# Token-major residual and block-product gates in a two-layer hybrid encoder on one core

## The chip, the cores and the metric

The kernel runs on one core of a Trainium2 chip. The metric is device time in microseconds of one execution; lower is better. The core's engines work side by side, each through its own list of instructions in a fixed order: TensorE (PE; PEld is its weight load), VectorE (DVE), ScalarE (ACT), GpSimd (POOL) and SyncE (SP), which here only starts transfers between DRAM and the on-chip memory. TensorE writes into eight banks of accumulation memory (PSUM), each 128 x 512 f32; the other engines read them out.

## What is computed

512 tokens, model width 1024, two layers. `w_in` has 7424 columns: five groups of branch A, two of branch B, queries, keys and values of branch C, and 3 x 1024 gate columns.

```python
xn = rms_norm(x, ln1[l])
z = xn @ w_in[l]
a_q, a_i, a_ff, a_fb, a_g, b_u, b_v, c_q, c_k, c_v, gz = jnp.split(z, offsets, axis=-1)
o_a = hgrn2_bidirectional(a_q, a_i, a_ff, a_fb, lower[l])
y_a = rms_norm(o_a, a_norm[l]) * silu(a_g)
y_b = spatial_gating(gelu(b_u), gelu(b_v), w_s[l], b_s[l])
y_c = window_attention(qh, kh, vh, sink[l])
gates = sigmoid(gz.reshape(bsz, s_len, 3, D_MODEL))
merged = (gates[:, :, 0] * (y_a @ w_br[l, 0])
          + gates[:, :, 1] * (y_b @ w_br[l, 1])
          + gates[:, :, 2] * (y_c @ w_br[l, 2]))
x = x + merged @ w_out[l]
hn = rms_norm(x, ln2[l])
x = x + square(relu(hn @ w_up[l])) @ w_down[l]
```

After both layers comes `rms_norm(x, final_norm)`. Branch A is a gated linear recurrence, forward and backward, in four heads.

## The kernel before

Line numbers are those of the kernel before unless said otherwise. Activations lie feature-major: a tile holds 128 features by 512 tokens (`xT`, `xcur`, eight tiles for the width). Each f32 operand of a large product is split into a rounded part and a rest (`xh`, `xl`; `wh`, `wl`), and a product is three matmuls (`mm3`, L144): L145, L146, L147. Weights come in chunks of 128 x 1024 f32 (512 KB) through `wload` (L114): SP loads `wr`, ScalarE casts `wh` (L123), VectorE subtracts `wl` (L125). `wr`, `wh` and `wl` have two buffers each. `proj` (L149) makes one feature-major tile from one chunk, 24 matmuls. `proj_tok` (L158) makes four token-major tiles of 128 tokens by 512 features; a_i (`vt`) and b_v (`bv`) use it.

A layer goes: head 0 of branch A; branch B; head 1; branch C; heads 2 and 3; then `merge_pass` (L599) for each branch. `merge_pass` projects the gate columns (`gz`, L608), scales them with the row `rb` of norms (L611), takes a tanh (L612), projects the branch (`y`, L615) and multiplies (L619 to L622). Then follow the output projection `wo` (L794), the residual, the second norm, and the MLP in four parts `qd`: eight `up` projections, and a `down` (L289). `down` works by a scheme of seven block products in place of eight: sums of quarter blocks of the weights (L327, L340, L822, L825) and of the activations (`left_sums`, L251) go in, and `take` adds each product into `acc`. At the end of a layer `acc` is scaled, transposed (`dT`, L835) and added to `xcur`; the next norm's squares are summed over partitions by matmuls (`colsum`, `cs`, L188), the power is taken on POOL (L198), and `rb` is spread by matmuls (`bcast`, L205).

A head (`a_gates`, L384, and `a_head`, L415) is a chain. `a_gates` makes `ex` (one buffer) and `key`. Then seven levels: ScalarE takes two exponentials of `ex` (`qt` L437, `kt` L443), VectorE multiplies (L438, L445), TensorE makes `at` in a bank of the tag "a", of which there is one (L422), VectorE or ScalarE copies it under a mask (L427, L460), and VectorE updates `ex` four times (L464). After the levels come the states (`kd`, `kT`, `stp`, `st`), the output `av`, a norm, a transpose `oT` (L520) and the scaled copy (L522). Branch C goes through 16 pairs of a score step (`c_scores`, L704) and an output step (`c_out`, L734).

A scheduler fixes the order of each engine's list when the kernel is built: it takes the program, the dependencies and priorities (`tc.high_priority`), and mixes stages where buffers allow. So in the kernel before the matmuls of `gz` and `y` stand among those of heads 1 to 3 and branch C. Banks: 3 of tag "m", 1 "a", 2 "c", 2 "s".

Of the kernel before, what the change touches and what calls it, by code (L numbers as in the profile page):

```python
# [32 lines left out]
def trunk(tc, xT, ws, vec, bsb, snk, wst, rope, cmask, amask, ident, out):  # L33
# [17 lines left out]
    SLOTS = {"x": 16, "h": 22, "l": 12, "z": 4, "rb": 1, "q": 2, "a": 3, "oa": 4, "yc": 4, "g": 3}  # L51
    BRANCH = ("q", "a", "oa", "yc", "g")

    part = {}
    BANKS = {"m": 3, "a": 1, "c": 2, "s": 2}
    WR, WB, NZ, NCT, NSM, NQ = 2, 2, 3, 4, 4, 10
# [5 lines left out]
    def T(tag, name, dt=F32):  # L62
        where = part["br"] if tag in BRANCH else sb
        return where.tile([P, S], dt, tag=tag, bufs=SLOTS[tag], name=nm(name))

# [46 lines left out]
    ready = []  # L112

    def wload():  # L114
        if ready:
            return ready.pop(0)
        i = cnt[0]
        cnt[0] += 1
        with hp():
            raw = sb.tile([P, CW], F32, tag="wr", bufs=WR, name=nm("wr"))  # L120
            nc.sync.dma_start(raw, ws[i])
            hi = sb.tile([P, CW], F32R, tag="wh", bufs=WB, name=nm("wh"))
            nc.scalar.copy(hi, raw)  # L123
            lo = sb.tile([P, CW], F32R, tag="wl", bufs=WB, name=nm("wl"))
            nc.vector.tensor_tensor(lo, raw, hi.bitcast(F32), ALU.subtract)  # L125
        return hi, lo

    def qload():

        i = cnt[0]  # L130
        cnt[0] += 1
        t = part["mlp"].tile([P, CW], F32, tag="wq", bufs=NQ, name=nm("wq"))
        with hp():
            nc.sync.dma_start(t, ws[i])
        return t
# [13 lines left out]
    def proj(xs, name, w=None, koff=0, nk=KT):  # L149

        hi, lo = w if w is not None else wload()
        pt = PT("m", name)
        for k in range(nk):
            c = slice((koff + k) * P, (koff + k + 1) * P)
            mm3(pt, hi[:, c], lo[:, c], xs[k][0], xs[k][1], k == 0, k == nk - 1)
        return pt

    def proj_tok(xs):  # L158

        pts = [PT(tag, "pm") for tag in ("m", "m", "c", "c")]  # L160
        for i in range(4):
            hi, lo = wload()
            for k2 in range(2):
                k = 2 * i + k2
                c = slice(k2 * S, (k2 + 1) * S)
                for t in range(4):
                    tt = slice(t * P, (t + 1) * P)
                    xh, xl = xs[k][0][:, tt], xs[k][1][:, tt]
                    nc.tensor.matmul(pts[t], xh, hi[:, c], start=k == 0, stop=False)
                    nc.tensor.matmul(pts[t], xl, hi[:, c], start=False, stop=False)  # L170
                    nc.tensor.matmul(pts[t], xh, lo[:, c], start=False, stop=k == 7)
# [39 lines left out]
    def norm_begin(which, l):  # L211
        n = Norm()
        n.which, n.l, n.acc, n.last, n.xs, n.k = which, l, None, None, [], 0
        return n

    def norm_add(n, xt, do_split=True, sq_pool=False):
        k = n.k
        n.k += 1
        if do_split:
            hi, lo = T("x", "xh", F32R), T("x", "xl", F32R)  # L220
            split(xt, hi, lo, ln_ap(n.which, n.l, k))
            n.xs.append((hi, lo))
        sq = T("z", "sq")
        if sq_pool:
            nc.gpsimd.tensor_tensor(sq, xt, xt, ALU.mult)
        else:
            nc.scalar.activation(sq, xt, AF.Square)
        if n.acc is None:
            n.acc = sq
        elif not do_split and k == KT - 1:  # L230
            n.last = sq
        else:
            a = T("z", "sqa")
            nc.vector.tensor_tensor(a, n.acc, sq, ALU.add)
            n.acc = a

    def norm_end(n, square=False):
        rc = rstd_c(colsum(n.acc, n.last), D)
        n.rc = rc
        if square:  # L240
            n.src = SM("r2", 4)
            nc.vector.tensor_tensor(n.src, rc, rc, ALU.mult)
            return
        pt = bcast(rc)
# [3 lines left out]

    HT = 2 * P

    def left_sums(h, u, nh):  # L251

        V = nc.vector

        def hl(n):
            res = []
            for _ in range(n):
                if nh[0] < 22:
                    res.append(T("h", "sh", F32R))
                else:  # L260
                    res.append(part["mlp"].tile([P, S], F32R, tag="hx", bufs=6, name=nm("hx")))
                nh[0] += 1
            return res

        def two(pr, i):
            return tuple(x[:, i * HT:(i + 1) * HT] for x in pr)

        if h is None:
            p1 = hl(1)[0].rearrange("p (a b) -> p a b", a=2)
            split(u[:, 0:HT], p1[:, 0], p1[:, 1])  # L270
            sb_ = part["mlp"].tile([P, 2, HT], F32, tag="sf", bufs=2, name=nm("sf"))
            V.tensor_tensor(sb_[:, 0], u[:, 0:HT], u[:, HT:], ALU.subtract)
            return {1: (p1[:, 0], p1[:, 1]), "u": u, "s": sb_}
        v, u, sb_ = u, h.pop("u"), h.pop("s")
        v_ = hl(2)
        split(v, *v_)
        a11, a21, a12, a22 = u[:, 0:HT], u[:, HT:], v[:, 0:HT], v[:, HT:]
        sa = part["mlp"].tile([P, 2, HT], F32, tag="sf", bufs=2, name=nm("sf"))
        V.tensor_tensor(sa[:, 0], a22, a21, ALU.subtract)
        V.scalar_tensor_tensor(sa[:, 1], sa[:, 0], -1.0, a11, ALU.mult, ALU.subtract)  # L280
        a_ = hl(2)
        split(sa.rearrange("p a b -> p (a b)"), *a_)
        V.scalar_tensor_tensor(sb_[:, 1], a12, -1.0, sa[:, 1], ALU.mult, ALU.subtract)
        b_ = hl(2)
        split(sb_.rearrange("p a b -> p (a b)"), *b_)
        h.update({2: two(v_, 0), 4: two(v_, 1), 5: two(a_, 0), 6: two(a_, 1), 7: two(b_, 0), 3: two(b_, 1)})
        return h

    def down(qd, raw, hs, acc):  # L289
        b11, b12, b22, b21, t1 = raw[0:2], raw[2:4], raw[4:6], raw[6:8], raw[8:10]  # L290
        V = nc.vector
        first = qd == 0
# [15 lines left out]
        def take(t, fl, pt, sign, fresh=False):  # L308
            d = acc[t][fl]
            with hp():  # L310
                if fresh:
                    nc.scalar.activation(d, pt, AF.Copy, scale=float(sign))
                else:
                    V.tensor_tensor(d, d, pt, ALU.add if sign > 0 else ALU.subtract)

        pa = [PT("c", "dA") for _ in range(2)]
        product(1, b11, pa, True)
        for p in range(2):
            take(p, 0, pa[p], 1, first)
        pb = [PT("m", "dB") for _ in range(2)]  # L320
        product(2, b21, pb, True)
        for p in range(2):
            take(p, 0, pb[p], 1)
        t2 = b11
        with hp():
            for s_ in range(2):
                V.tensor_tensor(t2[s_], t1[s_], b22[s_], ALU.add)  # L327
        product(6, t2, pa, False)
        for p in range(2):
            take(2 + p, 0, pa[p], 1, first)  # L330
        pc = [PT("m", "dC") for _ in range(2)]
        product(7, b12, pc, True)
        for p in range(2):
            take(2 + p, 1, pc[p], -1, first)
        product(5, t1, pa, False)
        for p in range(2):
            take(2 + p, 1, pa[p], -1)
        with hp():
# [638 lines left out]
```

## Time and profile before

| | us |
|---|---|
| median of 3 runs | 1780.0 (1779.02 to 1781.77) |
| the profiled execution, its time | 1779.92 |
| the profiled execution, span from first to last instruction | 1778.1 |
| VectorE busy | 1251.2 |
| ScalarE busy | 947.4 |
| DMA traffic | 163.64 MB, mean 92 GB/s |

The page gives busy time as a share of the span, a strip of 40 slices in tenths, and groups of instructions by line: busy time, mean duration, and idle time ahead of them with what ended it. Matmuls are pipelined, so the durations of neighbours overlap.

### The profile page before, as it was taken

Reading aid. Unit: us, or ns where it says so; the run is one execution under the profiler, and the core shown is the slowest. Engines: PE = TensorE matmul, PEld = TensorE weight load, DVE = VectorE, ACT = ScalarE, POOL = GpSimd, SP = SyncE. Lnnn points to the kernel's source line nnn. Section 1 sums busy time; section 2 is a strip of 40 time slices with the busy share of each in tenths; the row PEclk is TensorE's granted clock in tenths of the full one; section 3 lists DMA queues with packets and bytes.
Section 4 is the critical chain, followed back from the end, with each engine's and each line's share of the span. In section 5 each row is a group of like instructions: output and inputs, shape, how many; then the busy total and the mean of one; then the engine's idle time right before and its main releaser. Section 6 shows DMA issues by size and latency. Waiting matters only on the chain.

```text
span 1778.1 us, 21652 instructions
## 1 busy us (share of the span) xinstructions
PE 1728.6 (97%) x8128; PEld 1426.8 (80%) x8128; DVE 1251.2 (70%) x2053; ACT 947.4 (53%) x1568; POOL 93.5 (5%) x105
## 2 busy tenths in 40 slices
PE   7999999999999999999999999999999999999995
PEld 5788888888778887878788877888878788888884
DVE  5678968675655758586867897777655556677675
ACT  3664876543335554546565669675323364645454
POOL 3012000000000000000110210000000000000000
PEclk9999999999999999999999999999999999999997
DMA  4222212222622232232132211122243223141401
GB/s 171 83 83 72 75 57 72 72 89 83 219 95 95 84 118 92 99 119 71 66 113 83 84 60 60 62 69 78 95 183 119 94 73 127 63 142 61 141 12 48
DMA packets 46728, 163.64 MB, mean 92 GB/s; under 512 B 5664, under 2 KB 6176, under 8 KB 46624
## 3 DMA queue, kind: packets, MB, share of 16 engines
q1 hardware_dynamic: 43488, 152.82, 25.4%
q0 software_dynamic: 2560, 8.39, 1.4%
q8 instruction: 64, 1.05, 0.2%
q10 hardware_dynamic: 576, 1.05, 0.2%
q14 instruction: 40, 0.33, 0.1%
HBM read 158.05 MB, written 4.19 MB: 91 GB/s over the span
## 4 chain that ended last, share of the span: by engine, by line
PE 85%; DVE 7%; ACT 5%; issue 1%; DMA 1%; SPq 0%; POOL 0%; DVEq 0%; ACTq 0%
PE up L145 7%; PE up L146 7%; PE up L147 7%; PE gz L145 5%; PE gz L147 5%; PE gz L146 5%; PE dA L304 3%; PE dA L306 3%; PE dA L305 3%; PE at L422 3%; PE y L145 2%; PE y L147 2%; PE y L146 2%; PE dC L304 2%; PE po L749 2%; PE wo L147 2%
## 5 line engine op out<-in xcount | busy, mean ns | idle before, releaser
L123 ACT CAST wh<-wr 128x1024 fp32r<-128x1024 f32 x220 | 229.7, 1049 | 362.4 <-PE up L146 104.9
L125 DVE TENSOR_TENSOR wl<-wr,wh 128x1024 fp32r<-128x1024 f32 x220 | 269.0, 1224 | 188.0 <-ACT wh L123 178.1
L145 PE MATMUL up<-xh,wh 128*128 128x512 f32 x512 | 199.7, 390 | 0.1
L147 PE MATMUL up<-xh,wl 128*128 128x512 f32 x512 | 199.4, 389 | 0.0
L146 PE MATMUL up<-xl,wh 128*128 128x512 f32 x512 | 199.3, 389 | 0.0
L139 ACT CAST wh<-wq 128x1024 fp32r<-128x1024 f32 x112 | 117.5, 1049 | 152.0 <-PE dA L305 44.1
L141 DVE TENSOR_TENSOR wl<-wq,wh 128x1024 fp32r<-128x1024 f32 x112 | 136.4, 1221 | 49.4 <-ACT wh L139 49.1
L145 PE MATMUL gz<-xh,wh 128*128 128x512 f32 x384 | 152.6, 397 | 2.7 <-ACT wh L123 2.2
L147 PE MATMUL gz<-xh,wl 128*128 128x512 f32 x384 | 151.5, 395 | 1.6 <-DVE wl L125 1.5
L146 PE MATMUL gz<-xl,wh 128*128 128x512 f32 x384 | 151.5, 395 | 0.0
L145 PEld LDWEIGHTS up<-xh,wh 128*128 128x128 f32 x512 | 96.1, 188 | 21.6 <-ACT wh L123 1.7
L147 PEld LDWEIGHTS up<-xh,wl 128*128 128x128 f32 x512 | 96.1, 188 | 19.9
L146 PEld LDWEIGHTS up<-xl,wh 128*128 128x128 f32 x512 | 96.1, 188 | 19.9
L145 PEld LDWEIGHTS gz<-xh,wh 128*128 128x128 f32 x384 | 72.5, 189 | 18.2 <-ACT wh L123 4.1
L147 PEld LDWEIGHTS gz<-xh,wl 128*128 128x128 f32 x384 | 72.5, 189 | 17.4 <-DVE wl L125 3.2
L464 DVE TENSOR_TENSOR ex<-ex 128x256 f32<-128x256 f32 x224 | 85.6, 422 | 0.2
L146 PEld LDWEIGHTS gz<-xl,wh 128*128 128x128 f32 x384 | 72.5, 189 | 13.6
L304 PE MATMUL dA<-wh,sh 128*128 128x512 f32 x208 | 81.9, 394 | 0.5
L305 PE MATMUL dA<-wh,sh 128*128 128x512 f32 x208 | 81.1, 390 | 0.0
L145 PE MATMUL y<-yh,wh 128*128 128x512 f32 x192 | 75.4, 395 | 3.4 <-DVE z L575 1.8
L147 PE MATMUL y<-yh,wl 128*128 128x512 f32 x192 | 75.9, 396 | 0.0
L146 PE MATMUL y<-yl,wh 128*128 128x512 f32 x192 | 75.4, 392 | 0.0
(312 smaller groups left out, 3987.2 us busy)
## 6 DMA issues: line engine op xcount, KB each, us to landing
wr<-in_ws_dram SPq DMA_DIRECT2D x220, 512.0 KB, 3.2
wq<-in_ws_dram SPq DMA_DIRECT2D x64, 512.0 KB, 3.3
x<-in_xT_dram SPq DMA_DIRECT2D x8, 256.0 KB, 9.1
xr<-in_xT_dram POOLq DMA_DIRECT2D x8, 256.0 KB, 4.0
xspill<-xr POOLq DMA_DIRECT2D x8, 256.0 KB, 2.8
xr<-xspill POOLq DMA_DIRECT2D x8, 256.0 KB, 3.0
out_dram<-xf SPq DMA_DIRECT2D x4, 256.0 KB, 2.4
out_dram<-xf ACTq DMA_DIRECT2D x4, 256.0 KB, 2.3
```

The lines of the kernel that those rows point to most:

```text
L123: nc.scalar.copy(hi, raw)
L125: nc.vector.tensor_tensor(lo, raw, hi.bitcast(F32), ALU.subtract)
L139: nc.scalar.copy(hi, raw)
L141: nc.vector.tensor_tensor(lo, raw, hi.bitcast(F32), ALU.subtract)
L145: nc.tensor.matmul(pt, whi, xhi, start=first, stop=False)
L146: nc.tensor.matmul(pt, whi, xlo, start=False, stop=False)
L147: nc.tensor.matmul(pt, wlo, xhi, start=False, stop=last)
L304: nc.tensor.matmul(pts[p], xh[:, t], hi[:, c], start=start and k == 0, stop=False, skip_group_check=True)
L305: nc.tensor.matmul(pts[p], xl[:, t], hi[:, c], start=False, stop=False, skip_group_check=True)
L306: nc.tensor.matmul(pts[p], xh[:, t], lo[:, c], start=False, stop=k == 3, skip_group_check=True)
L422: nc.tensor.matmul(pt[:, c], kk(st), qq[:, c], start=True, stop=True)
L464: nc.vector.tensor_tensor(ap_of(ex, o_, d), ap_of(ex, o_, d), ap_of(ex, i_, z), ALU.add)
```

## The change

- *Layout.* The residual, the branch outputs after projection, the sum over branches and the output projection become token-major: four tiles of 128 tokens by two halves of 512 features. Norm sums then lie along a row (`norm_tok`: ScalarE squares with a running sum); scaled transposes `xT` give the feature-major operands (`turn`). The sum over branches is transposed once (`mT`) ahead of `wo`. After the last layer the output is scaled and stored token-major.
- *Block products.* a_i beside b_v, and the three gates, are four units of 1024 x 1024. Each goes through `seven`, the scheme that `down` used, with sums of the normed input made by `left_x`. They stand ahead of the branches of their layer. A unit's weights come through `uload` into the ten `wq` buffers.
- *Gates in DRAM.* The tanh of each gate tile is stored to DRAM (`thd`) by a POOL-issued transfer and loaded again in `gated`, which takes the place of `merge_pass`.
- *Order.* b_u of layer 0 comes first. The projections `ag` and the splits of branch B come behind the heads in the program. In the MLP, `done` adds the residual and starts the next norm as the products of the last part come out.

```diff
+def _chunk_keys():
...
+        res += [(l, "bu", i) for i in range(4)]
+        res += [(l, "un", u, q, i) for u in range(4) for q in range(4) for i in range(2)]
...
+    GROUPS = (("m", "m", "c", "c"), ("m", "a", "s", "s"))
...
+    def uload(*key):
+        raw = []
+        for i in range(10):
+            t = part["wq"].tile([P, CW], F32, tag="wq", bufs=NQ, name=nm("wq"))
+            if i < 8:
+                with hp():
+                    nc.sync.dma_start(t, ws[CHUNK[key + (i // 2, i % 2)]])
+            raw.append(t)
+        return [raw[2 * q:2 * q + 2] for q in range(5)]
...
+    def norm_tok(which, l, xr, keep):
...
+        def add(t, fl):
+            j = T("jk", "jk")
+            nc.scalar.activation(j, xr[t][fl], AF.Square, accum_out=n.ss[:, t * 2 + fl:t * 2 + fl + 1])
...
+        def turn(fl, ts):
...
+                pt = PT("s", "xT")
+                for i, t in enumerate(ts):
+                    nc.tensor.transpose(pt[:, i * P:(i + 1) * P], xr[t][fl][:, (d % 4) * P:(d % 4 + 1) * P], id_t)
...
+    def left_x(n):
+        res = []
+        for k in range(4):
+            h = {1: two(n.xs[k], 0), 2: two(n.xs[k + 4], 0), 4: two(n.xs[k + 4], 1)}
+            left_sums(lambda: T("xs", "xs", F32R), h, n.xf[k], n.xf[k + 4])
+            res.append(h)
+        return res
+    def early_sums(raw):
+        b11, b12, b22, b21, t1 = raw
+        for i in range(2):
+            nc.vector.tensor_tensor(t1[i], b11[i], b12[i], ALU.add)
+        for i in range(2):
+            nc.vector.tensor_tensor(b12[i], b12[i], b22[i], ALU.add)
+    def seven(raw, hs, name, on):
...
+        pa = [PT("c", name + "A") for _ in range(2)]
+        product(1, b11, pa, True)
+        read("P1", pa)
+        pb = [PT("m", name + "B") for _ in range(2)]
+        product(2, b21, pb, True)
+        read("P2", pb)
...
+        product(6, b11, pa, False)
+        read("P16", pa)
+        pc = [PT("m", name + "C"), PT("a", name + "C")]
+        product(7, t3, pc, True)
+        read("P7", pc)
+        product(5, t1, pa, False)
+        read("P165", pa)
...
+        product(4, b21, pc, False)
+        read("P74", pc)
+        product(3, b22, pa, False)
+        read("P1653", pa)
...
+            def keep(z, t, fl):
+                nc.gpsimd.dma_start(thd[:, br * 4 + t, fl * S:(fl + 1) * S], z)
...
+                elif which == "P1653":
+                    z = T("zt", "zt")
+                    A.activation(z, pt, AF.Tanh, scale=sc[:, 4 + p:5 + p])
+                    keep(z, p, 1)
+                else:
+                    z = w.pop(({"P2": "P1", "P165": "P7", "P74": "P16"}[which], p))
+                    V.tensor_tensor(z, z, pt, ALU.add)
...
+                    A.activation(z, z, AF.Tanh, scale=sc[:, c:c + 1])
+                    keep(z, t, fl)
...
+        for u in range(4):
+            nxt = uload(l, "un", u + 1) if u < 3 else None
+            seven(raw, hx, "t" if u == 0 else "g", on_tok if u == 0 else on_gate(u - 1))
+            if nxt:
+                early_sums(nxt)
+            raw = nxt
...
-        merge_pass(0, yb)
...
+        def gated(bi, br, ys):
+            nonlocal grp
+            for fl in range(2):
+                th = []
+                for t in range(4):
+                    z = T("th", "th")
+                    nc.gpsimd.dma_start(z, thd[:, br * 4 + t, fl * S:(fl + 1) * S])
+                    th.append(z)
+                pts = proj_tok(ys, f"y{br}", (l, "y", br, fl), grp)
+                grp ^= 1
+                for t in range(4):
+                    with hp():
+                        if bi == 0:
+                            mg[t][fl] = T("mg", "mg")
+                            nc.vector.scalar_tensor_tensor(mg[t][fl], th[t], 1.0, pts[t], ALU.add, ALU.mult)
+                        else:
+                            nc.vector.scalar_tensor_tensor(th[t], th[t], 1.0, pts[t], ALU.add, ALU.mult)
+                            nc.vector.tensor_tensor(mg[t][fl], mg[t][fl], th[t], ALU.add)
+                if bi == 2:
+                    for d in range(4 * fl, 4 * fl + 4):
+                        pt = PT("s" if grp == 0 else "c", "mT")
+                        for t in range(4):
+                            nc.tensor.transpose(pt[:, t * P:(t + 1) * P], mg[t][fl][:, (d % 4) * P:(d % 4 + 1) * P], id_t)
...
+        def done(which):
+            def block(ts, fl):
+                for t in ts:
+                    nc.vector.scalar_tensor_tensor(xr[t][fl], acc[t][fl], r2[:, t:t + 1], xr[t][fl], ALU.mult, ALU.add)
+                    n1.add(t, fl)
+                    if not last:
+                        nc.gpsimd.dma_start(xspill[:, t, fl * S:(fl + 1) * S], xr[t][fl])
+                if not last:
+                    n1.turn(fl, ts)
...
+    for fl in (0, 1):
+        for t in (2, 3, 0, 1):
+            nc.vector.scalar_tensor_tensor(xr[t][fl], xr[t][fl], n1.rc[:, t:t + 1], fn_t[fl], ALU.mult, ALU.mult)
+            (nc.scalar if t % 2 else nc.sync).dma_start(out[:, t, fl * S:(fl + 1) * S], xr[t][fl])
```

In the changed kernel's order, as built, the four units of a layer stand first; then all `f`, `q`, `ck`, `cv` and `cq` projections ahead of the end of head 0; then, between the ends of heads 0 and 3, the `ag` projections, a part of the `y` products of branch B, and the small matmuls of heads and attention. Each SP list starts with the first weights and the `x` tiles; in the changed kernel the first eight `wq` loads stand among the `x` tiles.

664 lines of the change are left out of this document (349 added, 315 removed).

## The prediction

> **What bounds the kernel now.** I read the busy shares first, then the slices, then the windows between the ends of the recurrence heads, then the groups by line, and the order of instructions on each engine last.
>
> ```profile
> PE 1728.6 (97%) x8128; PEld 1426.8 (80%) x8128; DVE 1251.2 (70%) x2053; ACT 947.4 (53%) x1568; POOL 93.5 (5%) x105
> PE   7999999999999999999999999999999999999995
> DVE  5678968675655758586867897777655556677675
> ```
>
> TensorE is busy in every slice but the first and last, so fewer matmuls shorten the kernel as long as TensorE stays fed. The 70% of VectorE is a mean over unlike stages; the windows separate them (columns: length, busy time and count of PE, PEld, DVE, ACT, POOL, then granted clock, DMA share, GB/s). The inner borders at 157.7 to 448.3 and 1024.6 to 1306 are ends of heads (the scaled copy of `oT`, L522).
>
> ```profile
> 0.00:157.70 157.70, 142.94 (x672) 117.09 (x673) 111.66 (x192) 77.39 (x114) 26.77 (x29) 0.98 0.31 105
> 157.70:256.70 99.00, 97.36 (x509) 82.36 (x509) 82.55 (x189) 72.96 (x154) 10.49 (x11) 1.00 0.20 69
> 256.70:356.20 99.50, 99.50 (x528) 84.98 (x526) 74.34 (x170) 61.79 (x151) 4.36 (x6) 1.00 0.21 69
> 356.20:448.30 92.10, 91.96 (x455) 76.81 (x454) 59.68 (x98) 36.56 (x67) 2.87 (x3) 1.00 0.26 83
> 552.00:877.70 325.70, 325.33 (x1426) 264.92 (x1425) 226.34 (x293) 170.99 (x230) 1.15 (x1) 1.00 0.26 88
> 1024.60:1123.60 99.00, 93.39 (x488) 77.92 (x487) 83.70 (x196) 77.48 (x167) 8.05 (x7) 1.00 0.18 59
> 1751.00:1778.10 27.10, 9.06 (x49) 7.64 (x46) 14.17 (x21) 9.78 (x18) 4.44 (x3) 0.65 0.20 78
> ```
>
> Heads are VectorE's heaviest stage: 82.55 of 99.00 us (83%) and 83.70 of 99.00 (85%). TensorE is still full there, because the gate and branch projections (`gz`, `y`) lie between the heads' small matmuls. That cover is what the change takes away.
>
> **What a matmul costs.** Durations overlap, so I take distances between starts.
>
> ```profile
> 1180.29 0.39 PE L145 MATMUL gz<-xh,wh 128*128 128x512 f32 x1
> 1180.51 0.39 PE L146 MATMUL gz<-xl,wh 128*128 128x512 f32 x1
> ...
> 1183.38 1.02 PE L749 MATMUL po<-pT,cvt 128*128 128x256 f32 x4
> 1184.24 0.49 PE L744 MATMUL pT<-id_t,sc 128*128 128x128 f32 x3
> 1184.48 0.36 PE L715 MATMUL sc<-k,q 128*128 128x256 f32 x1
> 1184.68 0.28 PE L716 MATMUL sc<-kl,q 128*128 128x256 f32 x1
> 1184.80 0.39 PE L145 MATMUL gz<-xh,wh 128*128 128x512 f32 x1
> ...
> 1185.50 0.83 PE L485 MATMUL stp<-vt,kT 128*128 128x128 f32 x6
> 1186.09 0.47 PE L145 MATMUL gz<-xh,wh 128*128 128x512 f32 x1
> ```
>
> A 512-wide matmul takes 0.2275 us (0.22 and 0.23 alternate), a transpose 0.08, a plain f32 128-wide matmul 0.2 (it shows as two), one `po` 0.43, a score pair 0.32.
>
> **The change, part by part.** Fewer matmuls: the gates and a_i/b_v took 768 matmuls of 512 columns per layer. As seven block products per unit they take 4 x 7 x 24 = 672. Saved: 192 x 0.2275 = 43.7 us. Token-major residuals and gates need 160 transposes (96 `xT`, 64 `mT`) where 64 `dT` were: 96 x 0.1 = +9.6 at the rate of the tail. The column sums and one broadcast that go are worth about -5. Net on TensorE: -39.
>
> The tail:
>
> ```profile
> 1750.84 1.04 PE L835 MATMUL dT<-id_t,acc 128*128 128x128 f32 x8
> 1764.12 0.16 DVE L196 TENSOR_SCALAR ms<-cs 128x4 f32<-128x4 f32 x1 [3.73 <-PE cs L191]
> 1764.36 1.01 POOL L198 TENSOR_TENSOR rs<-ms,mhalf_t 128x4 f32<-128x4 f32 x1 [335.29 <-DVE ms L196]
> 1768.15 5.83 DVE L851 TENSOR_TENSOR xf<-xf,rb 128x512 f32<-128x512 f32 x6 [3.87 <-ACT rb L246]
> ```
>
> From the last product to the end are now 27.5 us. After the change the transposes, column sum and broadcast are gone: two accumulates and two residual adds (4 x 0.68), a square 0.7, sums 0.4, the power 1.0, eight multiplies 5.1, handoffs about 1, and the 4.1 us that now follow the last multiply (1773.98 to 1778.1): 15. Gain 12; between 8 and 15.
>
> The heads without cover are the step that decides. In the changed order, TensorE has `f`, `q`, `ck`, `cv` and `cq` of all heads ahead of the end of the first head, and between the ends of the first and the last head of layer 0 only 96 `ag` and 84 `y` matmuls of 512 columns, instead of the gates as well. Its work there: 180 x 0.2275 = 41, 144 f32 matmuls (at, av, stp) 29, 35 `po` 15, 100 transposes 8, 22 score pairs, half of them 384 wide, 9: 102 us. In layer 1, 106. VectorE's work between the same two markers (310 and 328 instructions) comes from these rows:
>
> ```profile
> L464 DVE TENSOR_TENSOR ex<-ex 128x256 f32<-128x256 f32 x224 | 85.6, 422 | 0.2
> L438 DVE TENSOR_TENSOR qt<-qt,q 128x512 f32<-128x512 f32 x56 | 39.5, 705 | 10.1 <-ACT qt L437 9.7
> L445 DVE TENSOR_TENSOR kt<-kt,key 128x512 f32<-128x512 f32 x48 | 32.9, 685 | 10.6 <-ACT kt L443 10.6
> L427 DVE COPY_PREDICATED at<-amask_t,at 128x512 f32<-128x512 uint8 x40 | 29.5, 738 | 12.3 <-PE at L422 12.3
> L718 DVE CUSTOM_DVE_ANT_0 sc<-sc,cmask_t,snk_t 128x256 f32<-128x256 f32 (+1 forms) x64 | 34.7, 544 | 16.3 <-PE pT L744 16.0
> L125 DVE TENSOR_TENSOR wl<-wr,wh 128x1024 fp32r<-128x1024 f32 x220 | 269.0, 1224 | 188.0 <-ACT wh L123 178.1
> ...
> 292.21 0.76 DVE L464 TENSOR_TENSOR ex<-ex 128x256 f32<-128x256 f32 x2
> ```
>
> Layer 0: 83 `ex` 35, 21 `qt` and 18 `kt` 27, 15 masked copies 11, 24 scores 13, 7 weight splits 9, some 140 others of their own forms 44: 139 us of durations. Two `ex` take 0.76 where 2 x 0.42 stand, so about 8% is overlap: 128 us. Layer 1: 135. So even a VectorE that never waits exceeds TensorE's 102 and 106 by 26 and 29, 55 us together: the lower bound. It will wait, though: `ex` has one buffer, and the `at` bank is one, so a head's seven levels and its tail run in series, each crossing ScalarE, VectorE and TensorE, and the next head queues behind. VectorE's share in these stages is 85% at best and 65% at worst (59.68 of 92.10). At 65% the excess is 95 + 102 = 197, the upper bound. I take 85%, nearest to the head that runs beside the attention: 128/0.85 - 102 = 49 and 135/0.85 - 106 = 53, together +101. The stretch up to the end of the first head stays under TensorE: layer 0 has 433 matmuls of 512 columns there, 98 us, and 21 us of small ones, against 93 us of VectorE's rows.
>
> Smaller terms, with the rows that price them:
>
> ```profile
> 5.88 1.22 DVE L125 TENSOR_TENSOR wl<-wr,wh 128x1024 fp32r<-128x1024 f32 x1 [4.94 <-ACT wh L123]
> 11.63 1.23 DVE L125 TENSOR_TENSOR wl<-wr,wh 128x1024 fp32r<-128x1024 f32 x1 [3.09 <-ACT wh L123]
> ...
> 10.00:15.00 5.00, 3.19 (x7) 1.91 (x8) 3.37 (x3) 4.26 (x7) 3.17 (x2) 1.00 1.06 407
> ...
> xr<-xspill POOLq DMA_DIRECT2D x8, 256.0 KB, 3.0
> ...
> L612 ACT ACTIVATE gz<-gz 128x512 f32<-128x512 f32 x48 | 30.2, 628 | 3.5 <-DVE gz L611 3.4
> ```
>
> Start: SP now issues eight 512 KB `wq` loads between the `x` loads, and VectorE has four wide sums (1.22 each), ten half-width differences and four splits ahead of the last `xl`, some 13 us more; the 3.09 us that it waits after its first weights and a little besides take 4 of it, so +9 (0 to 13). Layer boundary: the transposed splits, 16 differences and eight splits for the sums, about 23 us of VectorE, must precede the third product; two products cover 11, and today's loss there is 2: +10 (0 to 14). Branch to gated sums: gate tiles come back from DRAM into space the heads free, 3 us per load, and eight multiplies of 0.68 must release a bank group before the next projection: +4 a layer, +8 (0 to 20). Unit to unit: the last product's two banks wait for two tanh of 0.63: 1.2 x 6, +7 (0 to 15).
>
> Costed at nothing: within a unit, 14 splits and 8 sums x 1.22 plus 6 adds x 0.68 are 31 us on VectorE against 168 x 0.2275 = 38 on TensorE, as in the window 552 to 877.7, where the MLP products run at 226.34 of 325.70 with TensorE full. Without that cover each unit would cost what VectorE lacks. The gates' way through DRAM adds 24 writes and 24 reads of 256 KB per layer; a unit then moves 4.2 MB of weights and 2.1 MB of gates in 38 us, 165 GB/s, and 407 were reached at the start. POOL issues these transfers in order with its own work, and the powers queued behind them are waited for at stage ends only.
>
> Sum, against the profiled execution's span: 1778.1 - 39 - 12 + 101 + 9 + 10 + 8 + 7 = 1862, plus the 1.8 us by which its time (1779.92) exceeds its span: 1864. That execution lies at the median, 1780.0. I round to **1862**.
>
> **Rivals.** (1) *TensorE stays the bound.* The heads' idle time stays below the 51 us saved, because VectorE's rows there shrink once no gate work is mixed in and the heads overlap each other: 1779.9 - 51 = 1729 with no idle time, some 1740 with a little. For it: 97% busy now, and 51 us that are certain. Against: the 55 is a sum of rows. It decides from the point where TensorE's added idle time, both layers, is under 51 us. Chance 0.10.
>
> (2) *The clock falls.* After TensorE sat idle, the same rows get slower:
>
> ```profile
> 1760.54 1.84 PE L188 MATMUL cs<-ones_t,sqa 128*128 128x1 f32 x8 [3.99 <-DVE sqa L234]
> 552.57 0.95 PE L188 MATMUL cs<-ones_t,sqa 128*128 128x1 f32 x8
> ```
>
> 1.84 against 0.95 for the same eight, clock 0.65 in the last window. If the gaps in the heads do this throughout, the work of 102 and 106 doubles to 204 and 212, over VectorE's 151 and 159: +106, 1970; for half of the time about 1915. Against: the heads' small matmuls come every microsecond or two. Chance 0.15. The Trainium skill ("TensorE: Matmul & The Clock Gate", "Part 1: The HAM clock gate") says that TensorE is throttled to half clock by default and after an idle window of about 3.4 us; the 3.99 us gap agrees with it, and by that rule the gaps that I expect would leave the clock up.
>
> (3) *The gates' return is the wait.* POOL's queue lets the loads go late, and each of the six gated groups of a layer waits for a landing of 3 us plus its multiplies, 12 x 6 = 72 in place of my 8: 1926. Against: eight buffers, loads ahead of use. Chance 0.05.
>
> **How the numbers follow.** Forecast 0.70, rivals 0.10, 0.15, 0.05. The forecast's own range is 1815 to 1915: its idle term at 100% (1818) up to near 72%. The range for eight in ten takes the floor with the small terms at nothing (1784) and half of the clock case with a few terms high: 1784 to 1930. About 0.2% is what a measurement can tell from no change. Faster by that needs rival 1: 0.10; within it 0.03; slower 0.87.
>
> **What would show it.** Right: TensorE busy 20 to 40% less than the length of the stretch between the first and last head ends (about 150 us long against 290 now), VectorE near 85% there, `at` and `qt` rows waiting for each other, and no idle time in the block products beyond a microsecond a unit; a tail near 15 us. Wrong: TensorE above 90% busy there, VectorE's rows shorter than today's, or the idle time in the block products or at the gate loads instead. A clock well under 1 in these stretches speaks for rival 2, idle time of `mg` rows behind DMA for rival 3.

## The result and the profile after

The changed kernel takes 1921.28 us (median of 4 runs, 1918.14 to 1922.46) against 1779.85 us for the kernel before beside it: ratio 1.079, 95% interval 1.0772 to 1.0809, so slower. The prediction was 1862: right in sign, and 59 us too low. The measured time lies 6 us beyond the forecast's own range (1815 to 1915) and inside its range for eight in ten (1784 to 1930). All line numbers below are those of the kernel whose rows are shown.

The page of the changed kernel, its busy times and three of its strips of 40 slices:

```profile
PE 1773.7 (92%) x7984; PEld 1435.0 (75%) x7984; DVE 1386.0 (72%) x2206; ACT 1028.4 (54%) x1707; POOL 142.6 (7%) x199
...
PE   6999999688699999999989999987887999999997
...
DVE  8887688677574676676887758986865657576867
...
PEclk7999999699699999999989999997997999999999
```

TensorE has 144 instructions fewer than before (7984 against 8128) and is busy for longer (1773.7 against 1728.6 us). The strip shows where: two dips of the PE line, slices 8 to 11 and 27 to 31, with lower digits of the granted clock under them. The windows put borders to that. Their columns are those of the prediction's windows; 340.2, 404.8, 465.2, 520.6 and 1283.1, 1348.2, 1411.3, 1464.8 are ends of the four heads of each layer (scaled copy of `oT`, L598).

```profile
0.00:48.40 48.40, 30.31 (x88) 20.38 (x88) 39.65 (x71) 23.49 (x35) 14.67 (x17) 0.79 0.61 223
48.40:218.70 170.30, 166.78 (x713) 133.24 (x714) 132.41 (x145) 97.49 (x123) 15.17 (x26) 0.99 0.32 108
218.70:340.20 121.50, 119.96 (x599) 100.45 (x597) 98.15 (x183) 74.78 (x123) 16.91 (x16) 1.00 0.28 91
340.20:404.80 64.60, 48.68 (x216) 40.72 (x217) 42.75 (x81) 29.62 (x54) 3.19 (x4) 0.74 0.10 33
404.80:465.20 60.40, 48.65 (x278) 38.57 (x277) 49.09 (x165) 48.76 (x151) 4.79 (x5) 0.97 0.03 9
465.20:520.60 55.40, 39.75 (x191) 33.20 (x190) 28.94 (x64) 22.59 (x59) 1.02 (x1) 0.77 0.06 20
520.60:623.60 103.00, 100.17 (x445) 80.94 (x446) 63.05 (x85) 33.20 (x49) 17.50 (x32) 0.97 0.48 169
...
966.20:1138.30 172.10, 166.74 (x701) 131.09 (x700) 132.73 (x153) 99.79 (x142) 19.48 (x29) 0.97 0.35 117
...
1464.80:1567.70 102.90, 100.63 (x444) 81.42 (x445) 63.11 (x85) 33.18 (x49) 17.16 (x32) 0.97 0.48 169
...
1907.20:1920.70 13.50, 0.00 (x0) 0.00 (x0) 7.75 (x14) 1.39 (x4) 1.01 (x1) 0.67 0.40 156
```

The stages that the prediction kept full are full: the block products (166.78 of 170.30) and the stretch of the first head (119.96 of 121.50). From the first to the last head end of layer 0 it is otherwise, and there VectorE is not full either: 42.75 of 64.60, 49.09 of 60.40, 28.94 of 55.40. The same two markers for both layers in one row each:

```profile
340.20:520.60 180.40, 137.09 (x682) 112.48 (x682) 120.79 (x308) 100.98 (x263) 8.99 (x10) 0.83 0.07 21
1283.10:1464.80 181.70, 136.94 (x702) 112.95 (x700) 123.61 (x318) 114.36 (x282) 8.89 (x10) 0.85 0.06 21
```

They last 362.1 us together. VectorE's share is 67% and 68%, where 85% had been taken. TensorE's 137 us are longer than its 102 and 106 us of work, in part because its mean clock was at 0.83 and 0.85: divided by that, the work would be 123 and 125 us. What makes up the rest was not traced.

VectorE's rows themselves kept their size (`ex`, now L540: 87.4 us against 85.6), and `at` waits for `kt`, as had been named. Two groups by line:

```profile
L498 PE MATMUL at<-qt,kt 128*128 128x128 f32 x448 | 75.5, 321 | 42.5 <-DVE kt L521 37.8
...
L540 DVE TENSOR_TENSOR ex<-ex 128x256 f32<-128x256 f32 x224 | 87.4, 434 | 0.1
```

Inside head 1, VectorE's rows of a level and the first of the next:

```profile
351.58 0.69 DVE L514 TENSOR_TENSOR qt<-qt,q 128x512 f32<-128x512 f32 x1 [0.69 <-ACT qt L513]
352.19 0.72 DVE L503 COPY_PREDICATED at<-amask_t,at 128x512 f32<-128x512 uint8 x1
352.80 0.68 DVE L521 TENSOR_TENSOR kt<-kt,key 128x512 f32<-128x512 f32 x1
353.39 1.43 DVE L540 TENSOR_TENSOR ex<-ex 128x256 f32<-128x256 f32 x4
355.52 0.69 DVE L514 TENSOR_TENSOR qt<-qt,q 128x512 f32<-128x512 f32 x1 [0.69 <-ACT qt L513]
```

A level comes every 3.94 us (351.58 to 355.52). VectorE waits in it once, 0.69 us for ScalarE's exponential, so it is busy for 3.2 of 3.94, 82%: near the 85%. The tail of a head is another matter. Head 3 of layer 0, TensorE's and VectorE's rows behind the last level:

```profile
500.12 2.07 PE L498 MATMUL at<-qt,kt 128*128 128x128 f32 x8 [2.53 <-DVE kt L521]
...
504.49 1.65 PE L561 MATMUL stp<-vt,kT 128*128 128x128 f32 x6 [0.57 <-ACT kT L558]
507.29 0.90 PE L556 MATMUL kT<-id_t,kd 128*128 128x128 f32 x3 [1.15 <-DVE st L568]
...
510.45 0.29 DVE L564 COPY st<-stp 128x128 f32<-128x128 f32 x1 [3.21 <-PE stp L561]
...
517.30 0.17 DVE L222 TENSOR_SCALAR ms<-ss 128x4 f32<-128x4 f32 x1 [5.79 <-ACT asq L589]
518.60 0.69 DVE L592 TENSOR_TENSOR ao<-av,rs 128x512 f32<-128x512 f32 x1 [1.13 <-POOL rs L224]
...
519.43 1.09 PE L596 MATMUL oT<-id_t,ao 128*128 128x128 f32 x4 [3.35 <-DVE ao L592]
```

and the window over them:

```profile
498.20:520.60 22.40, 12.79 (x50) 10.55 (x50) 6.92 (x17) 6.26 (x22) 1.02 (x1) 0.58 0.00 0
```

Every row waits for another engine, and each engine waits in turn; VectorE is busy for 6.92 of the last 22.4 us (31%). So a head without cover is some seven levels at VectorE's pace, and then some 20 us in which no engine is the bound. Head 1's tail is not bare in this way: the 96 `ag` projections stand among its steps in TensorE's order, and its second `kT` starts 11.7 us after its first `stp` (370.45 to 382.14), where head 3 takes 2.8 (504.49 to 507.29).

### The profile page after: what moved, and what is told of

It reads as the page before. It is cut to its first block, busy times and chain, and to the rows that moved or that the text cites. A ratio compares the mean times of both kernels' runs of the same rounds, so it can differ in the third digit from the quotient of the medians.

```text
span 1920.7 us, 22066 instructions
## 1 busy us (share of the span) xinstructions
PE 1773.7 (92%) x7984; PEld 1435.0 (75%) x7984; DVE 1386.0 (72%) x2206; ACT 1028.4 (54%) x1707; POOL 142.6 (7%) x199
## 3 DMA queue, kind: packets, MB, share of 16 engines
q10 hardware_dynamic: 576, 1.05, 0.1%
## 4 chain that ended last, share of the span: by engine, by line
PE 58%; issue 20%; DVE 13%; ACT 6%; DMA 1%; SPq 0%; POOL 0%; POOLq 0%; DVEq 0%; ACTq 0%
PE up L172 3%; PE up L170 3%; PE up L171 3%; PE gA L377 2%; PE gA L375 2%; PE gA L376 2%; PE y L197 2%; PE y L195 2%; PE at L498 2%; PE y L196 2%; DVE wl L166 2%; DVE ex L540 2%; PE wo L195 2%; PE wo L197 2%; PE wo L196 2%
## 5 line engine op out<-in xcount | busy, mean ns | idle before, releaser
L166 DVE TENSOR_TENSOR wl<-wq,wh 128x1024 fp32r<-128x1024 f32 x224 | 273.8, 1224 | 141.3 <-ACT wh L164 134.5
L164 ACT CAST wh<-wq 128x1024 fp32r<-128x1024 f32 x224 | 234.9, 1049 | 255.2 <-PE dA L376 54.0
L166 DVE TENSOR_TENSOR wl<-wr,wh 128x1024 fp32r<-128x1024 f32 x156 | 193.4, 1239 | 173.5 <-ACT wh L164 169.8
L164 ACT CAST wh<-wr 128x1024 fp32r<-128x1024 f32 x156 | 163.5, 1049 | 267.0 <-PE up L171 107.9
L498 PE MATMUL at<-qt,kt 128*128 128x128 f32 x448 | 75.5, 321 | 42.5 <-DVE kt L521 37.8
L498 PEld LDWEIGHTS at<-qt,kt 128*128 128x128 f32 x448 | 68.4, 228 | 50.2 <-issue 31.7
L377 PE MATMUL dA<-wl,sh 128*128 128x512 f32 x256 | 90.6, 394 | 0.0
L540 DVE TENSOR_TENSOR ex<-ex 128x256 f32<-128x256 f32 x224 | 87.4, 434 | 0.1
L195 PE MATMUL y<-wh,yh 128*128 128x512 f32 x192 | 79.8, 415 | 2.4 <-ACT on L598 1.6
L196 PE MATMUL y<-wh,yl 128*128 128x512 f32 x192 | 78.3, 408 | 0.0
L197 PE MATMUL y<-wl,yh 128*128 128x512 f32 x192 | 72.7, 407 | 1.6 <-DVE wl L166 1.6
```

The costliest lines, as they stand in the source:

```text
L377: nc.tensor.matmul(pts[p], xh[:, t], lo[:, c], start=False, stop=k == 3, skip_group_check=True)
L498: nc.tensor.matmul(pt[:, c], kk(st), qq[:, c], start=True, stop=True)
```

## The experiments

Twelve kernels, each an edit of the changed one (1921) or of the one named. e1_cover, e7_nounit, e10_align and e12_al are medians of four runs; the other eight are single runs, and the four runs of the changed kernel itself lie 4.3 us apart, so that a difference of 3 or 4 us in a single run shows nothing by itself. Theories: A, the heads' series of steps lost its cover; B, VectorE's amount of work; C, the gates' way through DRAM; D, the lower clock; E, the token-major parts; F and G, the start address of tiles or not.

| run | edit | us |
|---|---|---|
| e1_cover | gates beside the branches again | 1858.3 (1.0446, 1.0428 to 1.0463 against before) |
| e7_nounit | no block products ahead of the branches | 1803.3 (1.0125, 1.0108 to 1.0142) |
| e3_two | doubled buffers in a head, splits of branch B later | 1885.1 |
| e2_fill, e6_fill2, e13_tailclk | unread matmuls that hold the clock | 2019.2, 1947.3, 1911.1 |
| e5_nodram | gate tiles not stored and loaded | 1924.9 |
| e4_start | first weights started by POOL | 1918.2 |
| e11_half, e12_al | tiles moved by 384 and 128 bytes | 1908.6, 1908.5 (1.0725, 1.0707 to 1.0744) |
| e10_align | e7_nounit, tiles moved by 384 bytes | 1793.1 (1.0079, 1.0064 to 1.0094) |
| e14_sum | e3_two, e12_al and e4_start together | 1866.0 |

### The cover: e1_cover and e7_nounit

```diff
-        res += [(l, "un", u, q, i) for u in range(4) for q in range(4) for i in range(2)]
+        res += [(l, "un", 0, q, i) for q in range(4) for i in range(2)]
...
-        gated(0, 1, ys)
+        merge_pass(0, 1, yb, None)
```

> The changed kernel with one part undone: only a_i and b_v go as block products; the gates are projected feature-major beside the branch projections again, as before, without the way through DRAM; the token-major output projection, residual, MLP end and tail stay. Theory A (the heads lost their cover: their chain runs in series through single buffers and leaves TensorE idle about 154 us over both layers): 1921 - 154 idle + 144 x 0.2275 = 33 of matmuls that come back - 6 for 64 transposes mT that go = about 1795, between 1775 and 1815, and TensorE above 95% busy between the head ends. Theory B (VectorE is the bound between the head ends by the mere amount of its work): the gate rows come back onto VectorE there (24 scalings and 24 sums of 0.68 a layer), so this stretch gets no shorter than the work it then holds, and the whole stays above 1850. Theory C (the gates' way through DRAM is the wait): also near 1795, but the gain would have to stand at the gated sums, not between the heads.

Measured: 1858.3, half of what theory A expected. Its windows between the head ends of layer 0:

```profile
223.90:289.00 65.10, 50.77 (x216) 42.48 (x217) 39.33 (x76) 28.85 (x52) 3.23 (x5) 0.70 0.08 25
289.00:399.50 110.50, 110.50 (x584) 94.39 (x584) 79.72 (x201) 71.73 (x181) 4.02 (x5) 1.00 0.20 67
399.50:477.60 78.10, 75.28 (x381) 61.65 (x379) 53.41 (x97) 37.31 (x76) 3.55 (x6) 1.00 0.20 66
```

The first gate matmul, and TensorE's row ahead of it:

```profile
254.38 1.65 PE L563 MATMUL stp<-vt,kT 128*128 128x128 f32 x6 [0.57 <-ACT kT L560]
257.20 0.79 PE L172 MATMUL gz<-xh,wh 128*128 128x512 f32 x1 [1.18 <-DVE q L627]
```

Heads 2 and 3 are full again. Head 1 is as bare as in the changed kernel (65.1 us, clock 0.70): the one unit of block products ahead of head 0 had taken 45 us (48.6 to 93.7) in which no head ran, the `f`, `q` and `cq` projections were used up under head 0 alone, and the gates began only at 257.2, behind head 1's levels in TensorE's order and after a last wait of 1.18 us for VectorE's scaling of a `q`. So cover counts only where it stands beside the chain. Theory B's number, above 1850, came true, but not by its way: VectorE was busy for 39.33 of the 65.10 us of head 1, and heads 2 and 3, with the gate rows back on VectorE, are TensorE's.

e7_nounit takes the last unit out too:

```diff
-        for u in range(1):
-            seven(raw, hx, "t" if u == 0 else "g", on_tok)
+        vt = tok_tiles("vt", "vt", 0)
...
+        bv = tok_tiles("bv", "bv", 0)
```

> The changed kernel without any block products ahead of the branches: a_i, b_v and the gates are projected where the kernel before has them, head 0 starts at once, its b_u projection stands behind it again; the token-major output projection, residual, MLP end and tail stay. Theory A (the projections are the cover of the heads' chain, and block products ahead of head 0 use them up): TensorE above 95% busy from head 0 to the last head, and against the kernel before only the tail (-14), column sums (-5) and 32 more transposes (+3), and what wo and the MLP took longer in e1_cover (+8 a layer, the transposes among it): 1765 to 1785. Theory E (the token-major parts themselves cost what e1_cover is slower than before): 1820 or more.

```profile
154.90:440.60 285.70, 276.96 (x1421) 232.54 (x1420) 209.44 (x445) 165.84 (x357) 18.52 (x19) 0.99 0.20 68
1048.00:1336.60 288.60, 273.59 (x1385) 229.06 (x1385) 209.41 (x448) 174.63 (x366) 16.03 (x17) 0.98 0.20 66
```

Measured: 1803.3, 118 us under the changed kernel although 192 matmuls come back, with TensorE at 97% and 95% between the head ends. (The edit also takes out the costs of the units at the start and at their edges, so the 118 us are not the cover's alone.) The tail, 13.2 us, is the changed kernel's. It stays 23 us above the kernel before and 18 above the expectation: of these e10_align (below) explains 10, and the rest was not traced. Theory E, 1820 or more, falls.

### Single buffers: e3_two

```diff
-    BANKS = {"m": 3, "a": 1, "c": 2, "s": 2}
+    BANKS = {"m": 2, "a": 2, "c": 2, "s": 2}
...
-        ex = part["br"].tile([P, 4, S], F32, tag="ex", bufs=1, name=nm("ex"))
+        ex = part["br"].tile([P, 4, S], F32, tag="ex", bufs=2, name=nm("ex"))
```

> The changed kernel with the single buffers of a head doubled: bank tag a from 1 to 2 (m from 3 to 2), ex and at from one buffer to two, z2 from 3 to 4, the tag of qt and kt from 3 to 5; for the room, the splits of branch B come behind the last head (some 3 us a layer). Theory A (single buffers put heads in series): two heads run side by side, the stretch between first and last head end falls from 180 towards VectorE's 128 and 135 us of work, the whole by 40 to 90 us, to 1830-1880. Theory B (VectorE's amount of work): within 10 us of 1921.

```profile
319.00:477.80 158.80, 129.87 (x712) 108.94 (x710) 122.40 (x329) 111.48 (x285) 6.74 (x8) 0.92 0.10 34
1236.10:1411.00 174.90, 138.78 (x742) 116.08 (x740) 137.50 (x364) 129.60 (x315) 6.67 (x8) 0.92 0.10 31
```

Measured: 1885.1, 36 us less, just outside the weak end of what theory A named. The two stretches fall from 180.4 and 181.7 to 158.8 and 174.9 us, and VectorE's share rises from 67% and 68% to 77% and 79%. But TensorE's order changed with the edit, and the 36 us can't be put down to the buffers alone. Ahead of the end of head 0 stand 341 and 422 of the layer's projections of 512 columns in place of 432 and 522, and the stretches up to there, from the first `f`, fall by 25 and 24 us. Head 1 takes the moved ones beside its chain: 187 and 202 such matmuls in 65.5 and 79.5 us, where 109 and 114 stood in 64.6 and 65.1. And all `y` matmuls now stand behind the last head, so the way from its end to the first `wo` grows from 52.6 to 71.7 and 71.0 us. From the end of head 0 to the first `wo` the two layers took 233.0 and 234.2 us before the edit and 230.5 and 246.0 with it: what was gained is cover that came to stand beside head 1. Whether the doubled buffers alone would shorten a chain was not tested.

### The clock: e2_fill, e6_fill2, e13_tailclk

```diff
+            if h:
+                for wd in (S, 2 * P):
+                    nc.tensor.matmul(PT("m", "fill")[:, 0:wd], qt[:, 0:P], qt[:, 0:wd], start=True, stop=True)
```

> The changed kernel with matmuls added whose results nobody reads: in heads 1 to 3, a 512-wide and a 256-wide f32 matmul per level between qt and at, two 384-wide ones behind each stp. They only keep TensorE busy. Theory A (series of steps): the granted clock in the stretches between the head ends rises from 0.74-0.81 to above 0.95, at falls from about 2.04 to about 1.1 us, and the whole changes by -40 to +5 us, since at, kT, stp, av and oT are a part of the chain (about 10 us a head at the most). Theory D (the lower clock is the main part of what the prediction missed): -50 or more, to 1870 or less.

Measured: 2019.2. Neither theory foresaw it, and the run tells nothing of the clock: the added matmuls took their turns in the banks of tag m, and the `f` projections of heads 2 and 3, which had been done by 329.8 us, now ran until 471.6, behind head 1.

```diff
             pt = PT("a", "at")
+            if fq is not None:
+                fill(pt, fq, S)
+                fill(pt, fq, 2 * P)
```

> The changed kernel with unread matmuls again, now written into the very bank that the next real product overwrites, so that no bank is taken from the projections: in heads 1 to 3, a 512-wide and a 256-wide f32 matmul ahead of each level's at, and one or two ahead of kT, stp, av and oT. Theory A (VectorE is in series inside a level: in e1_cover its rows qt, masked copy, kt and four ex fill 3.2 of a 3.93 us period, and at hides behind them): granted clock above 0.95 in the stretches of heads 1 and 3, levels stay near 3.9 us, only the tails gain, 2 to 4 us a head: the whole -5 to -20, so 1901 to 1916. Theory D (the lower clock is what the prediction missed): levels fall to about 3 us, the whole by 40 or more, to 1880 or less.

Head 3 of layer 0 in e6_fill2, two levels of TensorE:

```profile
503.66 1.05 PE L506 MATMUL at<-qt,kt 128*128 128x128 f32 x8
...
507.56 1.05 PE L506 MATMUL at<-qt,kt 128*128 128x128 f32 x8
```

and VectorE's `qt` rows beside them:

```profile
501.47 0.68 DVE L522 TENSOR_TENSOR qt<-qt,q 128x512 f32<-128x512 f32 x1
...
505.38 0.68 DVE L522 TENSOR_TENSOR qt<-qt,q 128x512 f32<-128x512 f32 x1
```

`at` takes 1.05 us instead of 2.04, and the level still 3.91 us (501.47 to 505.38). In a level the clock is worth nothing: theory D falls there, because VectorE's four kinds of rows stand in series and `at` beside them. The whole rose by 26 us to 1947.3, which no theory gave; in the tails and beside branch C the added matmuls stood ahead of the real ones (the stretch of head 2, 60.4 us before, took 71.6, with 41 `y` matmuls in it in place of 13).

```diff
+        def fill(w_, *widths):
+            if h == 3:
+                for n in widths:
+                    nc.tensor.matmul(PT("c", "fill")[:, 0:n], w_[:, 0:P], w_[:, 0:n], start=True, stop=True)
```

> The changed kernel with unread f32 matmuls in head 3 alone, written into banks of tag c, which nothing else uses there: 512 and 256 wide ahead of each level's at, and 256-wide ones in the waits of the tail (behind kd, behind stp, behind av). In e6_fill2 such matmuls stood in the bank of the tail and added as much as the clock gave. Theory D for the tail alone: kT, stp, av and oT halve, 0.4 x 2 + 0.8 x 2 + 2.2 + 0.5 = 5.1 us less for head 3, whose stretch falls from 55.4 and 53.5 to about 50 and 48.5 us, the whole to about 1911; doubled for head 1 this is at most 20 us of what the heads cost. Theory A without the clock: the stretch stays within 2 us, the whole within 3 us of 1921.

Measured: 1911.1, the number that theory D gave, but not by its way. From the end of the last `at` to the end of `av` head 3 took 11.2 us (490.44 to 501.64) instead of 13.9 (502.19 to 516.09): 2.7 us for the clock, with added matmuls still standing between these steps. The head's stretch fell by 9.2 and 7.5 us, mostly because TensorE's order changed with the edit: the added matmuls use the banks of tag c, which the first group of `y` projections needs, and of the 58 `y` matmuls in head 3 of layer 0 some 30 moved behind the head's end and 27 from its first levels into its tail. In the changed kernel they stood ahead of `at`:

```profile
478.81 1.06 PE L498 MATMUL at<-qt,kt 128*128 128x128 f32 x8
...
480.80 0.39 PE L196 MATMUL y<-wh,yl 128*128 128x512 f32 x1
...
485.45 0.39 PE L195 MATMUL y<-wh,yh 128*128 128x512 f32 x1
485.68 1.05 PE L498 MATMUL at<-qt,kt 128*128 128x128 f32 x8
```

6.87 us between two `at` in place of 3.9. If the tails of heads 1 and 3 of both layers are each worth as much, the clock is some 4 x 2.7 = 11 us; this is an estimate from one head, and head 1's tail, which the `ag` projections fill, was not measured.

### The way through DRAM, and the start: e5_nodram, e4_start

```diff
-                nc.gpsimd.dma_start(thd[:, br * 4 + t, fl * S:(fl + 1) * S], z)
...
-                    nc.gpsimd.dma_start(z, thd[:, br * 4 + t, fl * S:(fl + 1) * S])
+                    nc.gpsimd.memset(z, 0.0)
```

> The changed kernel without the stores and loads of the gate tiles (zeros stand in their place, so the gates are left out of the output). Theory A: 0 to -12 us, so 1909 to 1921. Theory C (the gates' return is the wait): -50 or more, at the gated sums.

Measured: 1924.9, a little above theory A's range. Without 25 MB of traffic nothing is gained; theory C falls. In the changed kernel the loads take 5.1 us to landing, and the products of the first branch waited for them 2.1 us in all:

```profile
L921 DVE SCALAR_TENSOR_TENSOR mg<-th,y 128x512 f32<-128x512 f32 x16 | 10.6, 685 | 2.1 <-DMA th<-thd 2.1
```

and the transfers' median times to landing:

```profile
thd<-zt POOLq DMA_DIRECT2D x48, 256.0 KB, 2.6
th<-thd POOLq DMA_DIRECT2D x48, 256.0 KB, 5.1
```

```diff
             if i < 8:
-                with hp():
-                    nc.sync.dma_start(t, ws[CHUNK[key + (i // 2, i % 2)]])
+                if key == (0, "un", 0):
+                    nc.gpsimd.dma_start(t, ws[CHUNK[key + (i // 2, i % 2)]])
```

(For the other units the two removed lines stay in an else branch.)

> The changed kernel with the first unit's eight weight loads started by POOL instead of SP, so that SP's queue has the loads of x and of b_u alone. Term of the prediction: +9 us at the start from loads and VectorE's sums ahead of the normed input. If SP's order of issue is the cause, the first block product starts 5 to 10 us earlier than 48.4 us, and the whole is 1911 to 1916; if VectorE's sums or the transfers' own rate are, within 3 us of 1921.

Measured: 1918.2, 3.1 us less, which is no more than the changed kernel's own runs differ (their lowest is 1918.14). The trace is clearer: the first block product starts at 44.1 instead of 48.4 us, a little under the range named, and the first `f` behind the units at 216.5 instead of 218.7. So SP's order is some 4 us of the start's term, and about half of that is left behind the units.

### Start addresses: e10_align, e11_half, e12_al

In the changed kernel 512-wide matmuls on `yh`, `yi`, `h` and `xs` tiles come at a slower beat than those on `x` tiles, in e7_nounit too. The first and last row of 31 matmuls of `wo` in a row, in the changed kernel and then in e12_al:

```profile
1551.21 0.39 PE L196 MATMUL wo<-wh,mgl 128*128 128x512 f32 x1
...
1558.18 0.40 PE L196 MATMUL wo<-wh,mgl 128*128 128x512 f32 x1
```

```profile
1540.08 0.40 PE L198 MATMUL wo<-wh,mgl 128*128 128x512 f32 x1
...
1546.90 0.39 PE L198 MATMUL wo<-wh,mgl 128*128 128x512 f32 x1
```

30 distances: 6.97 / 30 = 0.2323 us, and 6.82 / 30 = 0.2273 us. All that differs is a spare tile (of 96 columns, 384 bytes, in e10_align and e11_half):

```diff
+    pad_t = pool(name="pad", bufs=1).tile([P, 32], F32, name="pad_t")
+    nc.vector.memset(pad_t, 0.0)
```

> The changed kernel with a spare tile of 128 bytes, which moves yh, yi, h, xs and wq from 384 bytes past a multiple of 512 to multiples of 512. Theory F: 0.2325 to about 0.2273, 3072 x 0.005 = 15 us less, so about 1906. Theory G: within 3 us of 1921.

> The changed kernel with the same spare tile of 384 bytes, which moves yh, yi, h, xs and wq from 384 to 256 bytes past a multiple of 512. Theory F: those matmuls fall from 0.2325 to about 0.2283, 3072 x 0.0042 = 13 us less, so about 1908. Theory G: within 3 us of 1921.

> e7_nounit with a spare tile of 384 bytes per partition ahead of the pools of yh, yi, h and wq, which moves their tiles from addresses of 128 bytes past a multiple of 512 to multiples of 512; nothing else differs. Seen so far: 512-wide matmuls follow one another at 0.2273 us where their operands lie in tiles that start at a multiple of 512 bytes (up, f, gz, on x at multiples of 512), at 0.2283 where they start 256 past one (y and dA of the kernel before), and at 0.2325 where they start 128 or 384 past one (y, wo, dA here). Theory F (the start address sets the rate): y, wo, dA, dB, dC fall to about 0.2275, 2304 x 0.005 = 11.5 us less, so about 1792. Theory G (something else in these products): within 3 us of 1803.

The start addresses are those of the programs as built; the tiles of `x` and of the split weights stay at multiples of 512 in all of them. Measured: 1908.5, 1908.6 and 1793.1, that is -12.8, -12.7 and -10.2 us; theory F. The mean distances between neighbouring starts (those under 0.26 us) of `wo` fell from 0.2323 to 0.2276 in e12_al and 0.2275 in e11_half, and of `dA` from 0.2320 to 0.2271 in both. So a start at 256 bytes past a multiple of 512 is as good as one at a multiple; the 0.2283 of the kernel before was not its address, as the expectation had it. Slow are those at 128 or 384 past; other offsets were not tried.

### Together: e14_sum

The edits are those of e3_two, e12_al and e4_start.

> The changed kernel with the buffers of e3_two, the start addresses of e12_al and the POOL-issued first weights of e4_start together. If these three are separate costs, -36 - 13 - 3 from 1921: about 1869. Theory A: the lack of cover remains, 80 us and more above e7_nounit's 1803 less its own address cost.

Measured: 1866.0 against 1869: the gains of the three edits add up, 55 us off where their sum was 52. 73 us remain above e10_align, whose tiles also start at multiples of 256 bytes and which has the cover; theory A had named 80 and more. No version here beats the kernel before; the nearest, e10_align, is 0.8% slower.

## Why the prediction was right, and where it was short

- *Sign and place.* The step named as deciding, heads without cover, decided. Giving the cover back, and the units' own edges with it, takes 118 us off (e7_nounit). The prediction calls `gz` and `y` the cover; of the 943 matmuls of 512 columns between the head ends of layer 0 in the kernel before, 204 were `f`, `q` and `cq` projections, and these too moved ahead of the end of head 0.
- *The heads, +101: mis-sized.* Against 102 and 106 us of TensorE's work the stretches took 180.4 and 181.7, so the term measured 78 + 76 = +154, 53 us more, inside its bounds of 55 and 197. The failing step was the choice of one share for VectorE, 85%, "nearest to the head that runs beside the attention". Three heads are in the stretch and only one runs beside the attention; in layer 0 the shares were 66%, 81% and 52%. (VectorE's work came out a little below the 128 and 135 that were summed: 121 and 124.) At 85% the measured work of the three heads would have taken 50, 58 and 34 us; they took 64.6, 60.4 and 55.4, so the miss lies in heads 1 and 3. 85% was near for the levels (82%) and for head 2, not for the tails at 31%. No window of the kernel before shows the price of a bare head: the one with 85% had TensorE busy for 93.39 of 99.00 us and the one with 65% for 91.96 of 92.10, so there the big matmuls for the most part set the length, not the chain. That the measured 67% and 68% lie near the 65% of the upper bound is chance. What makes the bare heads long was measured only in part: e13_tailclk gives about 11 us, an estimate, for the clock in the tails, and the 36 us of e3_two are doubled buffers and a changed order together; how the rest divides between handoffs and `ag` and `y` matmuls ahead of the chain's steps was not measured.
- *TensorE, -39.* The counts came out as worked out, but the price of 0.2275 did not hold for tiles off a multiple of 256 bytes: +12.8 (e12_al). This term stood nowhere in the sum.
- *Tail, -12.* 13.5 us where 27.1 stood: -13.6.
- *Start, +9.* The 80th matmul of 512 columns begins at 50.5 us instead of 40.5: +10.
- *Unit to unit and boundary, +7 and +10.* Layer 0 took 170.3 us for 696 matmuls of 512 columns and 16 of 128 (162 us), layer 1 172.1 for 672 and its transposes and broadcasts (156): +8 and +16, of which 2 each are the addresses (384 x 0.005). Left are 6.5 and 14, 20.5 for the predicted 17.
- *Branch to gated sums, +8.* 103.0 and 102.9 us for 396 matmuls and the transposes (94): +9 a layer, 2 of it addresses, so +14 for the predicted 8.
- *The sum.* These corrections are +53, +13, -2, +1, +3.5 and +6, some 75 in all, and the whole was 59 above the forecast. The kernel before had idle time of its own in stages that were rebuilt, which the sum took for work: by the prediction's windows and two more, 9 us between its head ends and 4 behind the last head of layer 1 (62.63 us of TensorE in 66.20). That leaves 62.
- *Costed at nothing.* In the four units of layer 0 VectorE has 132 us in 170 and TensorE is full; the gates' trip is free (e5_nodram). Both right.
- *Rivals.* (1) fell: 154 us of idle time and slow clock against the 51 saved. (2) The clock did fall, to 0.50 through five levels of head 1, but the work did not double in time: in the levels it stands beside VectorE's series. Its fact was right, its price wrong; that its time for half of the stretch, about 1915, lies near 1921 is chance, because with the clock held up (e6_fill2) the levels stayed at 3.91 us. No gap up to there was over 2.53 us, so what the prediction drew from the Trainium skill ("TensorE: Matmul & The Clock Gate", "Part 1: The HAM clock gate": throttled after an idle window of about 3.4 us), that the expected gaps would leave the clock up, was wrong; with the rule read as one on gaps, the trace does not agree with it. (3) fell with e5_nodram.

## What to carry to other kernels

Before work is taken out of a full engine, look at what it was filling: a chain of small steps that crosses engines takes as long as its steps, and its price is added up step by step, levels and tail apart; a stretch that big work fills does not show it. Big work is cover only where it stands beside the chain in the engine's order; done ahead of the chain it covers nothing, and ahead of a step in the queue it delays it. When tiles move to new pools, compare the beat of the same matmul before and after.

## What the runs showed of the hardware that was not expected

- In these runs the f32 matmuls of 512 columns came some 0.005 us apart more when a tile started 128 bytes past a multiple of 256 per partition: `wo` every 0.2323 us instead of 0.2273. It holds with the odd tile as the held operand (`wo` above) and as the streamed one (`y`: 0.2322 in e7_nounit, 0.2281 in e10_align). Over the whole kernel it is 12.8 us.
- The clock halves without a long gap. In the window of head 1's levels TensorE is busy for half the time, at half clock, and its longest wait is 2.53 us:

```profile
346.05:366.07 20.02, 10.23 (x40) 8.87 (x40) 15.10 (x33) 7.32 (x14) 0.00 (x0) 0.50 0.00 0
```

```profile
366.07 2.08 PE L498 MATMUL at<-qt,kt 128*128 128x128 f32 x8 [2.53 <-DVE kt L521]
```
